# Attention scores as two products over all 128 rows, and the band mask in fp32r

## The chip, the cores and the metric

The kernel runs on one core of a Trainium2 chip. The metric is the device time of one execution in microseconds (us), the median of the runs shown; the kernel before takes 1642.43 us.

## The reference, cut to what matters

A two-layer backbone works on 256 context tokens followed by 256 latent tokens, 1024 channels each, all in float32. Each layer has three mixers side by side (differential attention, a gated recurrence, windowed attention), gates that merge them, an output projection and a squared-ReLU MLP. The change touches the scores of the two attentions:

```python
def diff_weights(q, k, lam):                 # differential attention, 4 heads x 2 parts of 64 channels
    s = jnp.einsum('bqhcd,bkhcd->bhcqk', q, k) * (DIFF_DIM ** -0.5)
    p = jax.nn.softmax(s, axis=-1)
    return p[:, :, 0] - lam * p[:, :, 1]
...
band = jnp.abs(kj - SWA_BLOCK - qi) <= WINDOW      # windowed attention, 8 query heads, 2 key heads of 64
s_win = jnp.einsum('bqhgd,bkhd->bhgqk', qn, kw) * scale
s_win = jnp.where(valid, s_win, MASK_VALUE)
s_ctx = jnp.einsum('bqhgd,bkhd->bhgqk', qn, k_c) * scale
```

Context queries see the 256 context keys; latent queries see all 512. The second layer needs latent queries alone.

## The kernel before, in words

**Products of split numbers.** A dense product is computed to nearly float32 precision from fp32r operands: each operand is stored as a high part (rounded to fp32r) and a low part (what rounding left). `mm_cm` (L240 to L251) and `mm_tm` (L253 to L263) issue three products per 128 rows: high x high, high x low, low x high. `weights` (L197) loads blocks of weights over SyncE's queue (SP) and splits them: ScalarE rounds (L227), VectorE subtracts (L228).

**The score operands.** A head has 64 channels, and two heads (or two parts of a head) share one 128-row tile. After the dense product, `rope` turns the latent columns on POOL (L907 to L909). `stack_q` (L911) builds for each half c a tile S: in the rows of that half the high part of the query (L917), in the other 64 rows its low part (L918). `stack_k` (L920) builds for each half a tile K1[c] that holds the high part of the key in both row halves (ScalarE, L928 and L929), and one tile KL for both halves, in which the rows of half c hold the low part of key c (VectorE, L930).

**The scores.** `scores` issues two products into one PSUM bank: S against K1[c] over all 128 rows (L937), which sums high x high and low x high, and then the rows of half c of S against the same 64 rows of KL (L938), high x low. The moving operand has 512 columns for a latent query tile and 256 for a context tile. In `swa_unit` a latent tile gets a third product (L1075): an identity against a 128x128 band of 0 and -1e30, both kept in bf16 in the tile `half`, added onto the 128 key columns that the window cuts.

**What follows.** In `diff_head` VectorE takes the row maximum (L977), ScalarE the exponential (L898), VectorE normalizes and subtracts the two parts (L980 to L983), TensorE transposes the weights (L989), ScalarE copies them (L991), TensorE multiplies with the values (L1002). In `swa_unit` the same is done with L1079 (maximum), L1090 (scaling), L1097 (transposes), L1100 and L1102 (copies) and L1110 (values, 64 columns of weights each); ScalarE and VectorE write the output split in two (L1116, L1117).

**What sets the order.** The code is traced in program order with generators run in turn: `run` steps two heads alternately, `pipeline` holds two window units in flight. A scheduler then puts the instructions of each engine in one fixed order, by priority and a model of times; blocks under `hp()` have a higher priority. So dense products of the next stage (blocks of w_in, gates, branch projections) stand between the score products on TensorE. Each engine works through its order strictly. Key stacks, splits of weights (L228) and maxima share VectorE's one queue.

**Buffers.** `R` is a pool of 22 units of 128x512 words. `get(k)` takes the k neighbouring units that were freed longest ago. `acts` (L892) takes the split outputs of a mixer, four pairs of units. Stacks take one unit per tile.

Of the kernel before, what the change touches and what calls it, by code (L numbers as in the profile page):

```python
# [13 lines left out]
BF16 = mybir.dt.bfloat16  # L14
AF = mybir.ActivationFunctionType
ALU = mybir.AluOpType
# [96 lines left out]
class Net:  # L113
    def __init__(self, ctx, tc, ins, out):
        self.tc, self.nc = tc, tc.nc
        self.I, self.out = ins, out
        nc = self.nc
        cp = ctx.enter_context(tc.tile_pool(name="cp", bufs=1))
        pp = ctx.enter_context(tc.tile_pool(name="pp", bufs=1, space=PSUM))

        def const(n, cols, dt=F32):
            return cp.tile([128, cols], dt, tag=n, name=n)

        self.cst = const("cst", C_END)
        self.msk = const("msk", SMALL * 32 + 128, I32)
        self.half = const("half", 3 * 128, BF16)
        self.prm = const("prm", 96)
        self.bT = const("bT", 96)
        self.M = [const(f"M{l}", 96) for l in range(DEPTH)]
        self.CA = const("CA", 256)  # L130
        self.sb = const("sb", 128)
        self.sl = const("sl", 256)
        self.hn = const("hn", 256)
        self.snk = const("snk", 32)
        self.lam = const("lam", 4)
        self.oml = const("oml", 8)
        self.nhalf = const("nhalf", 8)
        self.ones = const("ones", 32)
        self.yss = const("yss", 20)
        self.sm_t = const("sm", 512)  # L140
        self.sm_i = 0
        self.raw = const("raw", RAWS * 1024)
        self.whl = const("whl", 2 * 4096)
        self.h = const("h", 2 * 8 * T)
        nf, nr = 33, 22
        self.arf = const("arf", nf * UNIT)
        self.arr = const("arr", nr * UNIT)
        self.A = Arena(self.arf, 0, nf)
        self.R = Arena(self.arr, 0, nr)
        self.x = {}  # L150
        self.last_dma = None
        self.fence = [0, 0, []]
        self.exps = []
        self.pumps = []
        self.rate = 1
        self.ps = [pp.tile([128, 512], F32, tag=f"b{i}", name=f"b{i}") for i in range(8)]
        self.nd, self.np = 2, 7
        self.di = self.mi = self.wi = self.ri = 0
        self.ident = self.cst[:, C_ID:C_ID + 128]
        self.hact = [(r32(self.h[:, k * T:(k + 1) * T]), r32(self.h[:, (8 + k) * T:(9 + k) * T]))  # L160
                     for k in range(8)]
# [25 lines left out]
    def set_fence(self, ops, skip, count):  # L187
        """the splits of weight blocks skip .. skip + count - 1 from here on are traced behind ops"""
        self.fence = [skip, count, ops]
# [7 lines left out]
    def weights(self, pieces, rope=0, dst=None):  # L197
        """a block of 2048 columns, loaded in halves; pieces(half): (view fn of the half, source AP); the first `rope`
        columns, in groups of 64 (axis, half, 16), are taken as (half, axis, 16)"""
# [42 lines left out]
    def mm_cm(self, ps, w, nk, cc, act, t0, n, kt0=0, start=True, stop=True):  # L242
        """ps[128 channels, n tokens] = w[:, cc:cc+128]^T act"""
        nc = self.nc
        hi, lo = w
        for k in range(nk):
            xh, xl = act[kt0 + k]
            wh, wl = hi[:, k, cc:cc + 128], lo[:, k, cc:cc + 128]
            nc.tensor.matmul(ps, wh, xh[:, t0:t0 + n], start=start and k == 0, stop=False)  # L249
            nc.tensor.matmul(ps, wh, xl[:, t0:t0 + n], start=False, stop=False)  # L250
            nc.tensor.matmul(ps, wl, xh[:, t0:t0 + n], start=False, stop=stop and k == nk - 1)  # L251

    def mm_tm(self, ps, w, nk, c0, n, act, tt, kt0=0, start=True, stop=True):  # L253
        """ps[128 tokens, n] = act[:, tt]^T w[:, c0:c0+n]"""
        nc = self.nc
        hi, lo = w
        for k in range(nk):
            xh, xl = act[kt0 + k]
            xh, xl = xh[:, tt * 128:tt * 128 + 128], xl[:, tt * 128:tt * 128 + 128]
            wh, wl = hi[:, k, c0:c0 + n], lo[:, k, c0:c0 + n]  # L260
            nc.tensor.matmul(ps, xh, wh, start=start and k == 0, stop=False)  # L261
            nc.tensor.matmul(ps, xh, wl, start=False, stop=False)  # L262
            nc.tensor.matmul(ps, xl, wh, start=False, stop=stop and k == nk - 1)  # L263

# [34 lines left out]
    def setup_mixers(self):  # L299
# [10 lines left out]
        nc.vector.tensor_copy(self.half[:, 0:128], self.ident)  # L310
        nc.vector.tensor_copy(self.half[:, 128:384], self.cst[:, C_BAND:C_BAND + 256])
# [57 lines left out]
    def ada_late(self, l, groups, ahead=2):  # L369
        """the groups of layer l on the vector engine; each step loads for a later one"""  # L370
# [22 lines left out]
    def ada_acc(self, raw, k, acc):  # L393
        """sums over k of w * silu(c), by partition, one for each stream"""
# [50 lines left out]
    def mvec(self, l, s, i):  # L445
        """stream s: 0 latents, 1 context"""
        return self.M[l][:, s * 48 + i * 8:s * 48 + i * 8 + 8]

# [1 line left out]
    def rstd(self, ms, cols, add=True):  # L450
        """ms: mean squares, to which EPS is added unless it is in them"""
# [6 lines left out]
    def scale_vecs(self, l, sub, q=None):  # L458
        """of all channel tiles, or of q and 4 + q"""
# [11 lines left out]
    def first_norm(self):  # L471
        """normalized and transposed x, channel tile k -> [128, 512]"""
# [40 lines left out]
    def first_blocks(self, offs, evacs):  # L513
        """the first blocks of w_in[0]; channel tiles q and 4 + q are multiplied as soon as their modulation is known"""
# [45 lines left out]
    def prenorm(self, tt, yb):  # L560
        """x[tt] / rms, transposed: the PSUM tiles of channels 0..511 and 512..1023"""
# [24 lines left out]
    def modulate(self, tt, sv, tiles, yb, ops=(), quick=False):  # L586
        """the tiles of prenorm() to the activation of tokens tt; traced behind ops"""
# [36 lines left out]
    def post(self, tt, y, yss):  # L624
        """x += y / rms, where y already holds the gains; yss [128, 5]: the shares of y's quarters in the mean
        square, and EPS"""
# [10 lines left out]
    def tm_out(self, w, r0, act, y, yss, seqs, add, gains=None, after=None):  # L637
        """y[tt] (+)= act^T w[r0:r0 + 1024]; seqs: lists of (tokens, column blocks) worked through in turn; with gains,
        the mean squares of y are taken and y becomes y * gains(tt)"""
# [28 lines left out]
    def hgrn_dense(self, l, w, hp):  # L668
        """heads 2 hp and 2 hp + 1"""
# [59 lines left out]
    def tm_pair(self, w, off, dst=None):  # L729
        """buffers, token tiles [128, 256] in them, and the function that fills those of a range"""  # L730
# [14 lines left out]
    def hgrn_head(self, l, hd, s, v, gn, ys):  # L745
        """generator: one step of the chain at a time"""
# [116 lines left out]
    def readout(self, ps, tiles, gain, ys):  # L863
        """per-tile rms norm of ps[128 tokens, tile, 128], gain, transpose, split"""
# [27 lines left out]
    def acts(self, n):  # L892
        bufs = [self.R.get(2) for _ in range(n)]
        return bufs, [(r32(b[:, 0:T]), r32(b[:, T:2 * T])) for b in bufs]

# [4 lines left out]
    def rope(self, t):  # L900
        """in place on the latent half of t [128, 512]; 64-row heads hold (half, axis, 16)"""
# [10 lines left out]
    def stack_q(self, t, c, t0):  # L912
        """rows 64 c of t -> [128, tokens] with the high part there and the low part in the other rows"""
# [7 lines left out]
    def stack_k(self, t):  # L921
        """high parts of both row halves, each doubled; low parts"""
        nc = self.nc
        K1 = [self.R.get(1) for _ in range(2)]
        KL = self.R.get(1)
        for c in range(2):
# [3 lines left out]
            nc.vector.tensor_tensor(out=r32(KL[own, :]), in0=t[own, :], in1=K1[c][own, :], op=ALU.subtract)  # L930
        return K1, KL

    def scores(self, ps, S, c, tt, K1, KL, nk, stop=True):
        nc = self.nc
        own = slice(64 * c, 64 * c + 64)
        q = slice(tt * 128, tt * 128 + 128)
        nc.tensor.matmul(ps[:, 0:nk], r32(S[:, q]), r32(K1[c][:, 0:nk]), start=True, stop=False)  # L937
        nc.tensor.matmul(ps[:, 0:nk], r32(S[own, q]), r32(KL[own, 0:nk]), start=False, stop=stop)  # L938
# [19 lines left out]
    def diff_head(self, l, hd, q, k, v, ys):  # L958
# [37 lines left out]
        for b in S + K1 + [KL]:  # L996
            b.free()
# [61 lines left out]
    def swa_unit(self, l, tt, gp, S, K1, KL, v, ys):  # L1059
        """heads 2 gp, 2 gp + 1 of both groups for one token tile; column order (kv, g)"""  # L1060
# [8 lines left out]
        for i in range(4):  # L1069
# [3 lines left out]
            if tt >= 2:  # L1073
                k0 = 384 if tt == 2 else 256
                nc.tensor.matmul(ps[:, k0:k0 + 128], self.half[:, 0:128],  # L1075
                                 self.half[:, (tt - 1) * 128:tt * 128], start=False, stop=True)
# [46 lines left out]
    def gates(self, l, j, bufs=()):  # L1123
        """left as they are where the exponentials of a mixer run beside them; branch() takes the sigmoid then"""
# [18 lines left out]
    def branch(self, l, j, ys, gates, merged, last):  # L1143
        """merged += gates * (ys^T w_branch[j])"""
# [37 lines left out]
    def cm_blocks(self, loads, q0, skew, evac, done=lambda b: None, also=None):  # L1182
        """two channel tiles per block; skew: the first two blocks take the context half first, also()
        follows them in each half"""
# [32 lines left out]
    def pipeline(self, gens, depth):  # L1217
        """starts one generator per round, at most `depth` at a time"""
# [10 lines left out]
    def layer(self, l):  # L1229
# [5 lines left out]
        # token mixer  # L1235
# [29 lines left out]
        for b in list(S.values()) + K1 + [KL, sv]:  # L1265
            b.free()
# [39 lines left out]
        # channel mixer  # L1306
# [97 lines left out]
```

## Time and profile before

| | us |
|---|---|
| median of 3 runs | 1642.43 |
| lowest, highest run | 1640.19, 1645.79 |
| span of the profiled execution, first to last instruction | 1638.2 |
| TensorE matmuls busy in that span | 1596.6 (97%) |
| VectorE busy | 1082.4 (66%) |
| ScalarE busy | 784.5 (48%) |
| GpSimd (POOL) busy | 387.9 (24%) |

The profile holds one execution; the time around its span is known from the runs, which lie 2.0 to 7.6 us above it. PE is TensorE's matmuls, PEld its loads of weights (the stationary operand), which can run beside matmuls, DVE is VectorE, ACT is ScalarE. Matmuls are pipelined, so the durations of neighbours overlap; the distance from one start to the next tells what one occupies. Lines like L938 are lines of the kernel before.

### The profile page before, as it was taken

The page shows a single profiled execution, that of the slowest core. Times are in us where ns is not written, and L with a number is a line of the kernel's source. Part 1 is how long each engine was busy: PE and PEld are TensorE (multiplying, and loading weights), DVE is VectorE, ACT ScalarE, POOL GpSimd, SP SyncE. Part 2 cuts the span into 40 slices and gives each one's busy share as a digit, 9 for nine tenths or more (in the row PEclk, how much of TensorE's full clock was granted, in tenths as well). Part 3 has the DMA queues.
Part 4 walks back from the last instruction along what each step waited for, and adds up shares of the span by engine and source line. Part 5 has one row for each costly group of instructions (what it writes and reads, how often), then busy time and mean ns, then how long its engine had stood idle before and what let it go on. Part 6 is the DMA issues. An engine that isn't in the chain of part 4 may idle for free.

```text
span 1638.2 us, 30088 instructions
## 1 busy us (share of the span) xinstructions
PE 1596.6 (97%) x11806; PEld 1395.9 (85%) x11806; DVE 1082.4 (66%) x1974; ACT 784.5 (48%) x1648; POOL 387.9 (24%) x419
## 2 busy tenths in 40 slices
PE   6999999999999999999999999999999999989998
PEld 4788888787777679989898989999898888989998
DVE  4655534676466568777878756877768787765555
ACT  4443433455444457533324235754446655666554
POOL 1142415050410000310202011364455350121001
PEclk9999999999999999999999999999999999999999
DMA  9723243323432335465565524432434253436552
GB/s 279 227 79 116 79 142 103 93 63 116 132 97 55 106 113 184 149 208 174 174 187 186 177 82 143 141 104 78 130 104 104 76 157 104 155 121 188 182 181 91
DMA packets 234270, 220.26 MB, mean 134 GB/s; under 512 B 24400, under 2 KB 226320, under 8 KB 234128
## 3 DMA queue, kind: packets, MB, share of 16 engines
q1 hardware_dynamic: 234128, 218.34, 43.6%
q8 instruction: 92, 1.51, 0.4%
q14 instruction: 50, 0.41, 0.1%
HBM read 217.26 MB, written 1.05 MB: 133 GB/s over the span
## 4 chain that ended last, share of the span: by engine, by line
PE 85%; DVE 5%; POOL 4%; DMA 2%; issue 2%; ACT 2%; SPq 0%; DVEq 0%; POOLq 0%; ACTq 0%
PE b L249 15%; PE b L251 15%; PE b L250 15%; PE b L261 9%; PE b L263 8%; PE b L262 8%; PE b L938 2%; DMA arf<-in_w_ada_dram 1%; PE b L937 1%; POOL arf L907 1%; POOL arf L797 1%; PE b L1110 1%; PE b L365 1%; PE b L1097 1%; DVE whl L228 1%
## 5 line engine op out<-in xcount | busy, mean ns | idle before, releaser
L228 DVE TENSOR_TENSOR whl<-raw,whl 128x512 fp32r<-128x512 f32 x588 | 432.9, 757 | 217.3 <-ACT whl L227 205.1
L227 ACT CAST whl<-raw 128x512 fp32r<-128x512 f32 x588 | 356.3, 619 | 253.3 <-PE b L263 111.9
L249 PE MATMUL b<-h,whl 128*128 128x512 f32 (+1 forms) x1296 | 448.2, 347 | 0.4 <-ACT arf L741 0.2
L251 PE MATMUL b<-h,whl 128*128 128x512 f32 (+1 forms) x1296 | 446.1, 345 | 0.8 <-DVE whl L228 0.6
L250 PE MATMUL b<-h,whl 128*128 128x512 f32 (+1 forms) x1296 | 444.1, 343 | 0.0
L249 PEld LDWEIGHTS b<-h,whl 128*128 128x128 f32 x1296 | 247.0, 191 | 33.1 <-issue 2.7
L251 PEld LDWEIGHTS b<-h,whl 128*128 128x128 f32 x1296 | 246.3, 190 | 31.7 <-issue 3.4
L250 PEld LDWEIGHTS b<-h,whl 128*128 128x128 f32 x1296 | 246.4, 190 | 28.6 <-issue 3.3
L261 PE MATMUL b<-whl,arr 128*128 128x256 f32 x768 | 217.2, 284 | 0.0
L262 PE MATMUL b<-whl,arr 128*128 128x256 f32 x768 | 217.1, 283 | 0.0
L263 PE MATMUL b<-whl,arr 128*128 128x256 f32 x768 | 215.6, 283 | 1.0 <-DVE arr L1321 1.0
L1320 POOL TENSOR_TENSOR arf<-arf 128x256 f32<-128x256 f32 (+1 forms) x68 | 63.9, 939 | 425.1 <-ACT arr L1319 421.5
L261 PEld LDWEIGHTS b<-whl,arr 128*128 128x128 f32 x768 | 147.3, 192 | 1.3 <-DVE arf L653 0.8
L263 PEld LDWEIGHTS b<-whl,arr 128*128 128x128 f32 x768 | 146.6, 192 | 1.4 <-DVE arr L1321 1.4
L262 PEld LDWEIGHTS b<-whl,arr 128*128 128x128 f32 x768 | 147.4, 192 | 0.1
L261 PE MATMUL b<-whl,h 128*128 128x256 f32 x512 | 145.6, 286 | 0.0
L262 PE MATMUL b<-whl,h 128*128 128x256 f32 x512 | 145.4, 285 | 0.0
L263 PE MATMUL b<-whl,h 128*128 128x256 f32 x512 | 144.2, 285 | 0.0
L907 POOL TENSOR_TENSOR arf<-arf,cst 32x256 f32<-32x256 f32 x104 | 93.7, 901 | 204.9 <-DVE arf L983 80.9
L455 POOL TENSOR_TENSOR sm<-sm,nhalf 128x1 f32<-128x1 f32 (+2 forms) x42 | 32.3, 773 | 348.6 <-DVE sm L630 257.6
L404 DVE SCALAR_TENSOR_TENSOR arf<-arf,CA 128x1024 f32<-128x1024 f32 x84 | 110.0, 1355 | 5.3 <-DMA arf<-in_w_ada_dram 5.3
L261 PEld LDWEIGHTS b<-whl,h 128*128 128x128 f32 x512 | 97.8, 192 | 3.6 <-issue 1.2
(224 smaller groups left out, 2493.8 us busy)
## 6 DMA issues: line engine op xcount, KB each, us to landing
raw<-in_w_in_dram SPq DMA_DIRECT2D x110, 512.0 KB, 3.7
arf<-in_w_ada_dram SPq DMA_DIRECT2D x80, 512.0 KB, 4.7
raw<-in_w_mlp_down_dram SPq DMA_DIRECT2D x72, 512.0 KB, 3.9
raw<-in_w_mlp_up_dram SPq DMA_DIRECT2D x64, 512.0 KB, 3.8
raw<-in_w_out_dram SPq DMA_DIRECT2D x24, 512.0 KB, 3.4
arf<-in_w_ada_dram SPq DMA_DIRECT2D x32, 256.0 KB, 5.8
raw<-in_w_branch_dram SPq DMA_DIRECT2D x16, 512.0 KB, 3.7
raw<-in_w_in_dram SPq DMA_DIRECT2D x32, 128.0 KB, 2.9
```

What stands on the lines that cost most here:

```text
L227: self.behind(ops, lambda: nc.scalar.copy(r32(h), src))
L228: self.split_op = self.behind(ops, lambda: nc.vector.tensor_tensor(out=r32(l), in0=src, in1=h, op=ALU.subtract))
L249: nc.tensor.matmul(ps, wh, xh[:, t0:t0 + n], start=start and k == 0, stop=False)
L250: nc.tensor.matmul(ps, wh, xl[:, t0:t0 + n], start=False, stop=False)
L251: nc.tensor.matmul(ps, wl, xh[:, t0:t0 + n], start=False, stop=stop and k == nk - 1)
L261: nc.tensor.matmul(ps, xh, wh, start=start and k == 0, stop=False)
L262: nc.tensor.matmul(ps, xh, wl, start=False, stop=False)
L263: nc.tensor.matmul(ps, xl, wh, start=False, stop=stop and k == nk - 1)
L404: self.nc.vector.scalar_tensor_tensor(out=a[:, :], in0=raw[:, :], scalar=ca[:, k, s:s + 1], in1=a[:, :], op0=ALU.mult, op1=ALU.add)
L907: nc.gpsimd.tensor_tensor(out=b[o, 0:LAT], in0=x[i], in1=self.cst[i, C_RS:C_RS + LAT], op=ALU.mult)
L938: nc.tensor.matmul(ps[:, 0:nk], r32(S[own, q]), r32(KL[own, 0:nk]), start=False, stop=stop)
L1320: nc.gpsimd.tensor_tensor(out=r[:, c], in0=r[:, c], in1=r[:, c], op=ALU.mult)
```

## The change

`stack_k` makes two tiles KL[c] in place of one, each with the low part of key c in both row halves, which takes four subtractions per stack instead of two. The second score product then takes all 128 rows of S against all 128 rows of KL[c]; it adds low x low, which was left out before. The identity and the band are stored in fp32r in place of bf16. `acts` takes its four pairs as one block of eight units. Comments and docstrings are removed throughout; all lines move.

```diff
-        self.half = const("half", 3 * 128, BF16)
+        self.half = const("half", 3 * 128)
...
-        nc.vector.tensor_copy(self.half[:, 0:128], self.ident)
-        nc.vector.tensor_copy(self.half[:, 128:384], self.cst[:, C_BAND:C_BAND + 256])
+        nc.vector.tensor_copy(r32(self.half[:, 0:128]), self.ident)
+        nc.vector.tensor_copy(r32(self.half[:, 128:384]), self.cst[:, C_BAND:C_BAND + 256])
...
     def acts(self, n):
-        bufs = [self.R.get(2) for _ in range(n)]
-        return bufs, [(r32(b[:, 0:T]), r32(b[:, T:2 * T])) for b in bufs]
+        b = self.R.get(2 * n)
+        return [b], [(r32(b[:, 2 * i * T:(2 * i + 1) * T]), r32(b[:, (2 * i + 1) * T:(2 * i + 2) * T])) for i in range(n)]
...
     def stack_k(self, t):
         K1 = [self.R.get(1) for _ in range(2)]
-        KL = self.R.get(1)
+        KL = [self.R.get(1) for _ in range(2)]
         for c in range(2):
             own, oth = slice(64 * c, 64 * c + 64), slice(64 - 64 * c, 128 - 64 * c)
             nc.scalar.copy(r32(K1[c][own, :]), t[own, :])
             nc.scalar.copy(r32(K1[c][oth, :]), t[own, :])
-            nc.vector.tensor_tensor(out=r32(KL[own, :]), in0=t[own, :], in1=K1[c][own, :], op=ALU.subtract)
+            for o in (own, oth):
+                nc.vector.tensor_tensor(out=r32(KL[c][o, :]), in0=t[own, :], in1=K1[c][own, :], op=ALU.subtract)
         return K1, KL

     def scores(self, ps, S, c, tt, K1, KL, nk, stop=True):
         nc = self.nc
-        own = slice(64 * c, 64 * c + 64)
         q = slice(tt * 128, tt * 128 + 128)
         nc.tensor.matmul(ps[:, 0:nk], r32(S[:, q]), r32(K1[c][:, 0:nk]), start=True, stop=False)
-        nc.tensor.matmul(ps[:, 0:nk], r32(S[own, q]), r32(KL[own, 0:nk]), start=False, stop=stop)
+        nc.tensor.matmul(ps[:, 0:nk], r32(S[:, q]), r32(KL[c][:, 0:nk]), start=False, stop=stop)
...
-                nc.tensor.matmul(ps[:, k0:k0 + 128], self.half[:, 0:128],
-                                 self.half[:, (tt - 1) * 128:tt * 128], start=False, stop=True)
+                nc.tensor.matmul(ps[:, k0:k0 + 128], r32(self.half[:, 0:128]),
+                                 r32(self.half[:, (tt - 1) * 128:tt * 128]), start=False, stop=True)
```

Where the stacks are freed, `K1 + [KL]` becomes `K1 + KL`.

## Rows read from the trace of the kernel before

**Rows 1.** The page: busy time, share of the span and instructions of each engine.
```profile
PE 1596.6 (97%) x11806; PEld 1395.9 (85%) x11806; DVE 1082.4 (66%) x1974; ACT 784.5 (48%) x1648; POOL 387.9 (24%) x419
```

**Rows 2.** Windows: busy us of each engine per stretch, granted clock, DMA share, GB/s.
```profile
280.00:600.00 320.00, 319.73 (x1653) 236.75 (x1652) 189.57 (x402) 150.61 (x340) 51.84 (x62) 1.00 0.32 96
1225.00:1405.00 180.00, 177.55 (x1247) 152.50 (x1246) 136.53 (x259) 107.76 (x237) 58.43 (x67) 1.00 0.38 109
1230.00:1280.00 50.00, 48.84 (x310) 41.07 (x309) 42.68 (x72) 30.21 (x65) 23.93 (x26) 1.00 0.37 95
```

**Rows 3.** Matmul timeline: start, duration, line, out and in, shape; among ordinary products.
```profile
1240.25 0.40 PE L937 MATMUL b<-arr 128*128 128x512 f32 x1
1240.48 0.28 PE L251 MATMUL b<-h,whl 128*128 128x256 f32 x1
1240.60 0.28 PE L249 MATMUL b<-h,whl 128*128 128x256 f32 x1
```

**Rows 4.** Matmul timeline around two score groups of layer 0's windowed attention.
```profile
477.14 0.39 PE L251 MATMUL b<-arr,whl 128*128 128x512 f32 x1
477.46 0.50 PE L938 MATMUL b<-arr 64*128 64x512 f32 x1
477.89 0.23 PE L1075 MATMUL b<-half 128*128 128x128 bf16 x1
477.93 0.47 PE L937 MATMUL b<-arr 128*128 128x512 f32 x1
478.33 0.49 PE L938 MATMUL b<-arr 64*128 64x512 f32 x1
478.75 0.50 PE L249 MATMUL b<-arr,whl 128*128 128x512 f32 x1
479.09 0.39 PE L250 MATMUL b<-arr,whl 128*128 128x512 f32 x1
```

**Rows 5.** Timeline of weight loads (PEld) in the same stretch, with idle time before.
```profile
476.91 0.19 PEld L251 LDWEIGHTS b<-arr,whl 128*128 128x128 f32 x1
477.45 0.18 PEld L938 LDWEIGHTS b<-arr 64*128 64x128 f32 x1 [0.35 <-issue]
477.88 0.10 PEld L1075 LDWEIGHTS <-half 128*128 128x128 bf16 x1 [0.25 <-issue]
```

**Rows 6.** Instructions of line L938, and its engine's idle time ahead (us, times).
```profile
L938 PE MATMUL b<-arr x96: 277/492/502, 290.2 to 1383.0; 64*128 64x512 f32 x64, 64*128 64x256 f32 x32
...
  issue: 20.1, 71
```

**Rows 7.** Matmul timeline, a second score product of 256 columns in layer 0.
```profile
296.88 0.38 PE L938 MATMUL b<-arr 64*128 64x256 f32 x1
297.19 0.44 PE L989 MATMUL b<-cst,arf 128*128 128x128 f32 x2
297.38 0.48 PE L249 MATMUL b<-arr,whl 128*128 128x512 f32 x1
```

**Rows 8.** Matmul timeline, 128-column f32 products of layer 0.
```profile
341.45 0.61 PE L1002 MATMUL b<-arf 128*128 128x128 f32 x4
341.90 0.60 PE L989 MATMUL b<-cst,arf 128*128 128x128 f32 x4
```

**Rows 9.** Instructions of line L930: ns min/median/max.
```profile
L930 DVE TENSOR_TENSOR arr<-arf,arr x20: 672/689/1218, 276.3 to 1303.5; 64x512 fp32r<-64x512 f32 x20
```

**Rows 10.** VectorE and matmul timeline, where a stack ends close ahead of its scores.
```profile
313.16 0.69 DVE L930 TENSOR_TENSOR arr<-arf,arr 64x512 fp32r<-64x512 f32 x1
...
314.52 0.28 PE L937 MATMUL b<-arr 128*128 128x256 f32 x1
```

**Rows 11.** Matmul and ScalarE timeline: last read, first write of a mixer's outputs.
```profile
501.44 0.39 PE L251 MATMUL b<-arr,whl 128*128 128x512 f32 x1
...
510.61 0.27 ACT L1116 CAST arr<-b 128x128 fp32r<-128x128 f32 x1 [2.86 <-PE b L1110]
```

**Rows 12.** Windows, columns as in the second group: a stretch with stops.
```profile
1410.00:1450.00 40.00, 34.76 (x260) 33.37 (x259) 32.38 (x68) 25.46 (x62) 7.75 (x9) 0.92 0.48 152
```

More of the change, by code (lines that the diff above doesn't have):

```diff
@@ L13 @@
 I32 = mybir.dt.int32
-BF16 = mybir.dt.bfloat16
 AF = mybir.ActivationFunctionType
@@ L995, in diff_head @@
             yield
-        for b in S + K1 + [KL]:
+        for b in S + K1 + KL:
             b.free()
@@ L1264, in layer @@
         self.pipeline([self.swa_unit(l, tt, gp, S, K1, KL, sv, ys_c) for tt in reversed(tts) for gp in range(2)], 2)
-        for b in list(S.values()) + K1 + [KL, sv]:
+        for b in list(S.values()) + K1 + KL + [sv]:
             b.free()
```

## The prediction

> **What bounds the kernel now.** I read the busy shares first: TensorE's matmuls fill 97% of the span and VectorE 66% [rows 1]. As an average says little of a stage, the two attention stretches were cut out by windows: 280 to 600 us (layer 0) and 1225 to 1405 us (layer 1). TensorE is busy for 319.73 of 320 us and for 177.55 of 180 us, at a granted clock of 1.00, its upper level of 2.4 GHz [rows 2]. So there the matmul queue sets the pace: what a product occupies is paid, and what is taken from it comes back unless another engine is then late. VectorE is the next, and tightest in layer 1's differential attention, 42.68 of 50 us [rows 2].
>
> "Busy" hides how well the queue is filled, so the matmul timeline is read by the distance from one start to the next. A 512-column product on 128 rows costs 0.23 us among ordinary ones, a 256-column one 0.12 (1240.25 to 1240.48 to 1240.60, [rows 3]); that first product is L937 itself. Where L938 on 64 rows comes in, three distances grow [rows 4]: the one before it from 0.23 to 0.32 (477.14 to 477.46), its own to 0.43 (477.46 to 477.89), and that of the next full product to 0.34 (478.75 to 479.09). The weight loads say why: an ordinary load starts with the product before its own (the load at 476.91 serves the product of 477.14), while L938's starts at 477.45 with its product, after 0.35 us of idle [rows 4, 5]. The load queue was so held up ahead of 71 of the 96 L938, 20.1 us in all [rows 6].
>
> **The change part by part.**
> *Second score product on 128 rows (L938).* It keeps its 512 or 256 columns and its weights become the same 128x128 block that L937 loads. Its price becomes L937's among ordinary products, 0.23 or 0.12. Saved per product of 512 columns: 0.09 ahead + 0.20 of its own + 0.11 behind = 0.40. With 256 columns its own distance is 0.31 (296.88 to 297.19) instead of 0.12 [rows 7]; with 0.09 ahead and 0.10 behind, taken from the case of 512, that is 0.38. L938 is issued 96 times, 64 at 512 and 32 at 256 columns [rows 6]: 64 x 0.40 + 32 x 0.38 = 37.8. Where transposes follow instead of a product no delay is seen behind (297.19, two of them in 0.19 us, [rows 7]); I count 11 such places or ones followed by products of 32 or 64 columns, and take off 11 x 0.10 = 1.1. That leaves 36.7 us.
>
> *Band product in fp32r (L1075, 32 times: 2 token tiles x 2 x 4 heads x 2 layers).* It occupies 0.04 now (477.89 to 477.93) [rows 4]. No 128-column fp32r product is in the trace. Below, it stays at 0.04; above, it costs as much as a 512-column one, 0.23. I take the 128-column f32 products, four in 0.45 us, 0.11 each [rows 8]: they have its shape and an element as wide. So +0.07 x 32 = 2.2 us, between 0 and 6. Its weight load grows from 0.10 us towards the 0.19 of the load at 476.91 [rows 5]; I cost that at nothing, since an ordinary load lies beside the product before it. If that cover were gone it would cost 32 x 0.09 = 2.9 us. The Trainium skill (TensorE: Matmul & The Clock Gate, Weight-path perf modes) says that fast weight loading is for 128 weights of a type other than FP32; by it this part gives up a fast load. The two load lengths agree with that.
>
> Freed on the matmul queue: 36.7 - 2.2 = 34.5, say **34 us**.
>
> *Two more subtractions per key stack (L930).* Ten stacks get 20 more VectorE instructions of 64x512, median 0.69 and at most 1.22 us [rows 9] (the long ones fall where POOL runs rope): 14 to 24 us of VectorE time, for the most part beside other work. They also push back what is queued behind them, weight splits (L228) and the maxima (L977) for which exp waits. Mostly the stack ends well ahead of its scores. In some places it is close: the subtraction that starts at 313.16 ends at 313.85 and the first score of 256 columns follows at 314.52 [rows 10], 0.67 us, against 1.4 us added. Layer 1's differential stage, with 42.68 of 50 us, holds six of today's 20 and so gets six more, 4.1 to 7.3 us, while TensorE there gets faster; the work can slide into 1280 to 1300 us in part. I let 5 us come back as new waits there and in two or three close places; bounds none, and half of the 24.
>
> *Low parts in two buffers, outputs of a mixer in one block of eight units.* Going through the allocator's rule by hand, the pool of 22 units holds at most 20 at once in the attention stages. The outputs of the window attention now lie wholly on those of the differential attention; three of their four pairs did so before. The last product that reads these starts at 501.44 and the first write comes at 510.61 [rows 11], 9 us later. No cost. The setup's two casts and the removed comments: nothing.
>
> **Sum.** 34 - 5 = 29 us off the span of 1638.2, which gives 1609.2. The median shown lies 4.2 us above that span, so 1613.4: **1613 us**.
>
> **Rivals.**
> *Half goes into new waits.* TensorE, 7% faster in these stretches, meets the chain of maximum, exp and scaling that its own slowness covers now. For it: VectorE's share of 85% in one stage and the 0.67 us gap. Against it: today's idle time is 0.27 us in 320 and 2.45 in 180 [rows 2], so most results arrive well ahead. It gives back 17 us: 1625, between 1618 and 1635.
>
> *The full-height product is held up as well, so nothing is freed.* If a weight load could go ahead only beside a product on other rows, L938 would keep its 0.43 us; with the wider load and the band product 5 us would be added: 1647. Against it stand the ordinary products, all on 128 rows, whose loads do start one product ahead [rows 5]. The Trainium skill (TensorE: Matmul & The Clock Gate, The mechanism) has a rule of this kind, that loads overlap running matmuls only where the row group differs; the trace disagrees, with loads on the same 128 rows at a distance of 0.23 us.
>
> *Slower: the key stacks stop TensorE and its clock falls.* If at each of the ten stacks TensorE stood for both added subtractions at their longest, that is 10 x 2.44 = 24 us. Stops cost more than themselves: in 1410 to 1450 us TensorE idles 5.24 us and the mean granted clock is 0.92 [rows 12]; 16% of 40 us at 1.2 GHz instead of 2.4 would be 6.4 us, up to 3.2 of them lost, 0.6 per idle us. So 24 x 1.6 = 39 us against the 34: 1642.4 + 5 = 1647. It decides from 3.4 us per stack on, a stop of 2.1 us and its clock. Against it: all stacks but a few have other products queued between.
>
> **Chances.** Forecast 0.70, half given back 0.18, nothing freed 0.04, stops and clock 0.08; the last two shared out between no change (0.06) and slower (0.06). What can be told from no change here is 0.3%, 5 us. Faster 0.88. Range: below, 36.7 us with a band product at 0.04, no new wait and some us of scatter, 1601; above, half given back with a part of its spread, 1631.
>
> **What would show it.** L938's weight loads with no "issue" idle ahead of them; L938 at 0.23 to the next start, the product behind it too; L1075 at 0.11; L930 40 times; TensorE's idle time in the two stretches up by less than 5 us, at a clock of 1.00. The prediction is wrong if L938's loads still start with their products, or if the stretches, shorter in matmul time, are filled with waits for L930, L977 or L228.

## The result, and the profile after

The changed kernel takes **1622.66 us** (median of 4 runs, 1621.37 to 1623.33); the kernel before takes 1641.31 beside it (4 runs, 1639.38 to 1645.79). The ratio is 0.9884, with a 95% interval of 0.9868 to 0.9900: 18.7 us faster. Three executions of the runs below took 1932 us or more, in a slower state, and the medians leave them out. The forecast of 1613 was 9.7 us too low; the time lies inside the range and 2.3 us from the rival "half goes into new waits" (1625). Lines of the changed kernel carry the number of before minus one from L228 on (L936 and L937 are the two score products, L1074 the band), save for L930, the subtraction, which keeps its own.

First the page of the changed kernel, its busy times, which answer to [rows 1]:

```profile
PE 1569.2 (97%) x11806; PEld 1401.7 (86%) x11806; DVE 1091.5 (67%) x1994; ACT 782.5 (48%) x1648; POOL 387.8 (24%) x419
```

TensorE is busy 27.4 us less. The span, 1638.2 before and 1620.9 now, fell by only 17.3, so 10.1 us of the gain came back as idle time: span minus busy time was 41.6 and is 51.7.

**The score products did what was forecast.** The lines of L937 and L930 after (nanoseconds are minimum, median, maximum), which answer to [rows 6, 9]:

```profile
L937 PEld LDWEIGHTS b<-arr x96: 187/190/193, 289.8 to 1365.5; 128*128 128x128 f32 x96
L937 PE MATMUL b<-arr x96: 278/391/474, 289.9 to 1365.7; 128*128 128x512 f32 x64, 128*128 128x256 f32 x32
its engine sat idle before it (us, times) until:
...
L930 DVE TENSOR_TENSOR arr<-arf,arr x40: 674/687/1247, 275.6 to 1292.3; 64x512 fp32r<-64x512 f32 x40
```

Under "sat idle before it" nothing is left, where 20.1 us of "issue" in 71 places stood before. The matmul timeline after, around two score groups of layer 0's windowed attention, answers to [rows 4]:

```profile
470.99 0.39 PE L250 MATMUL b<-arr,whl 128*128 128x512 f32 x1
471.22 0.39 PE L937 MATMUL b<-arr 128*128 128x512 f32 x1
471.44 0.22 PE L1074 MATMUL b<-half 128*128 128x128 f32 x1
471.50 0.45 PE L936 MATMUL b<-arr 128*128 128x512 f32 x1
471.79 0.40 PE L937 MATMUL b<-arr 128*128 128x512 f32 x1
472.02 0.39 PE L248 MATMUL b<-arr,whl 128*128 128x512 f32 x1
472.25 0.39 PE L249 MATMUL b<-arr,whl 128*128 128x512 f32 x1
```

Read by starts, the product ahead of L937 takes 0.23 (470.99 to 471.22), L937 itself 0.22 and 0.23, the product behind it 0.23 (472.02 to 472.25). All three of the delays of before (0.32, 0.43, 0.34) are gone. The band product takes 0.06 and the product behind it 0.29, that is 0.06 over an ordinary one.

**Where the rest went** is read from the windows of the changed kernel. The columns are those of [rows 2]; the first two stretches are the two attention stretches at their new place, the next three lie inside them:

```profile
280.00:590.00 310.00, 305.76 (x1678) 242.21 (x1677) 200.04 (x422) 152.52 (x345) 52.93 (x62) 0.99 0.34 100
1209.00:1389.00 180.00, 171.37 (x1270) 159.15 (x1269) 141.15 (x271) 109.75 (x243) 60.37 (x69) 0.98 0.40 111
320.00:330.00 10.00, 7.68 (x35) 4.99 (x34) 9.89 (x24) 7.63 (x21) 0.72 (x1) 0.98 0.51 115
330.00:340.00 10.00, 10.00 (x43) 8.20 (x42) 4.50 (x7) 1.92 (x5) 8.67 (x12) 0.84 0.00 0
1250.00:1260.00 10.00, 5.62 (x33) 5.62 (x34) 9.71 (x17) 5.79 (x10) 4.16 (x5) 0.66 0.01 2
```

TensorE idles 4.24 us in the first stretch and 8.63 in the second, against 0.27 and 2.45 [rows 2]. In both bad places VectorE is full, 9.89 and 9.71 of 10 us, and the granted clock drops (0.84 behind the first, 0.66 in the second). In the first place TensorE's stops are short, 2.3 us in six; they end with exponentials (L897, four times), a scaling (L982) and an instruction of ScalarE (L951), and two of the exponentials had themselves waited for VectorE's maxima.

The largest stop stands in layer 1's differential attention. The matmul timeline after:

```profile
1247.81 0.28 PE L262 MATMUL b<-whl,h 128*128 128x256 f32 x1
1254.38 1.11 PE L988 MATMUL b<-cst,arf 128*128 128x128 f32 x4 [6.29 <-DVE arf L982]
...
1255.51 0.41 PE L261 MATMUL b<-whl,h 128*128 128x256 f32 x1
1255.72 0.42 PE L262 MATMUL b<-whl,h 128*128 128x256 f32 x1
...
1258.22 0.28 PE L262 MATMUL b<-whl,h 128*128 128x256 f32 x1
1258.34 0.28 PE L260 MATMUL b<-whl,h 128*128 128x256 f32 x1
```

In TensorE's order the transposes come next, and it waits 6.29 us for their input, the last scaling of the softmax (L982). After the stop a 256-column product takes 0.21 (1255.51 to 1255.72) instead of 0.12: the granted clock is at its lower level, 1.2 GHz, until 1258.1. That is twelve distances, 12 x 0.09 = 1.1 us. The four transposes and the product behind them take 1.13 (1254.38 to 1255.51) where 0.45 [rows 8] and 0.12 would do, another 0.5 or so. The stop and its clock cost 7.9 us in all.

Why L982 is so late stands on VectorE's timeline of the same stretch:

```profile
1242.15 0.68 DVE L976 TENSOR_REDUCE sm<-b 128x1 f32<-128x512 f32 x1
1246.02 1.56 DVE L916 CAST arr<-arf 64x256 fp32r<-64x256 f32 x2 [3.19 <-POOL arf L908]
1247.61 0.90 DVE L917 TENSOR_TENSOR arr<-arf,arr 64x256 fp32r<-64x256 f32 x1
1248.54 0.17 DVE L979 RECIPROCAL sm<-sm 128x2 f32<-128x2 f32 x1
...
1249.40 1.48 DVE L916 CAST arr<-arf 64x256 fp32r<-64x256 f32 x2
1250.92 0.90 DVE L980 TENSOR_SCALAR arf<-arf,sm,lam 128x512 f32<-128x512 f32 x1
1251.85 1.69 DVE L917 TENSOR_TENSOR arr<-arf,arr 64x256 fp32r<-64x256 f32 x2
1253.58 0.75 DVE L982 SCALAR_TENSOR_TENSOR arf<-arf,sm 128x512 f32<-128x512 f32 x1
```

and on ScalarE's, where the sum of the exponentials, the reciprocal's input, is read out:

```profile
1242.87 0.69 ACT L897 ACTIVATE arf<-b,sm 128x512 f32<-128x512 f32 x1 [2.42 <-DVE sm L976]
1243.45 0.19 ACT L897 ACTIVATION_READ_ACCUMULATOR arf<-b,sm 128x1 f32 x1
```

The reciprocal could have run at 1243.6. In VectorE's fixed order it stands behind two casts and a subtraction of the next heads' query stack, the first of which (L916) waits 3.19 us for POOL's rope (L908). Five more instructions of that stack stand ahead of the two scalings (L980, L982). None of L930 is in this chain.

**By stage.** The first product of each score pair (L937 before, L936 after) cuts the timeline into stages, from the start of the first such product to that of the last. They repeat to about 0.1 us from run to run where nothing was changed (once to 0.4); the setup (289 to 294 us to the first score) and the stretch between the layers (642 to 646) scatter by more than that. "Freed" is counted from distances of starts, the medians of before minus those of after: 0.40 for a 512-column product; 0.38 with 256 columns in the differential attention (0.09 ahead, 0.19 own, 0.10 behind) and 0.29 on average in the windowed one; 0.31 where a band product follows (0.09 ahead, 0.20 own, 0.02 for the band and what is behind it).

```
us, first to last score pair        before   after   change   freed by distances       given back
layer 0 differential                111.09  105.62    -5.5    16x0.40 + 16x0.38 = 12.5       7.0
layer 0 windowed                    108.45   99.11    -9.3    16x0.31 + 16x0.29 =  9.6       0.3
layer 1 differential                 67.39   68.88    +1.5    16x0.40           =  6.4       7.9
layer 1 windowed                     44.21   39.78    -4.4    16x0.31           =  5.0       0.6
all the rest                        1307.1  1307.5    +0.4                                   0.4
```

Less 1.1 for the places where transposes follow, 32 us were freed, and about half of it came back: the windowed attention kept its gain, the differential attention lost most of it.

### The profile page after: what moved, and what is told of

The parts are those of the page before. It is cut to its first block, busy times and chain, and to the rows that moved or that the text cites. A ratio compares the mean times of both kernels' runs of the same rounds, so it can differ in the third digit from the quotient of the medians.

```text
span 1620.9 us, 30093 instructions
## 1 busy us (share of the span) xinstructions
PE 1569.2 (97%) x11806; PEld 1401.7 (86%) x11806; DVE 1091.5 (67%) x1994; ACT 782.5 (48%) x1648; POOL 387.8 (24%) x419
## 4 chain that ended last, share of the span: by engine, by line
PE 84%; DVE 4%; POOL 4%; DMA 2%; ACT 2%; issue 2%; SPq 1%; DVEq 0%; POOLq 0%; ACTq 0%
PE b L248 15%; PE b L249 15%; PE b L250 15%; PE b L260 9%; PE b L261 9%; PE b L262 9%; DMA arf<-in_w_ada_dram 1%; POOL arf L906 1%; PE b L364 1%; POOL arf L796 1%; PE b L1109 1%; PE b L936 1%; PE b L1096 1%; DVE whl L227 1%; PE b L937 1%
```

## The experiments

Two accounts of the loss stood against each other. One: the added subtractions cost it, as work or through the order that they bring about. The other: a faster TensorE runs into VectorE's chain whether or not subtractions are added. Each run below changes what its title says (with two low tiles the block of eight goes along, as the pool then needs it); times are medians, ratios are to the kernel before on the same chip.

**The block of eight units alone.**

```diff
     def acts(self, n):
-        bufs = [self.R.get(2) for _ in range(n)]
+        b = self.R.get(2 * n)
...
```

> Kernel before, with the outputs of a mixer in one block of eight units and nothing else. All theories: the placement is free, 1641 us, within 5 us, with TensorE's starts as before (L938 at 0.43 us). If placement or the new order that the scheduler makes of it counts, it moves by more than 5 us either way.

1640.59, ratio 0.9997 [0.9988, 1.0006]. It costs nothing, as forecast; the windowed stage of layer 0 stays at 108.45 us.

**The band in fp32r alone**, beside second score products on 64 rows as before.

```diff
-        self.half = const("half", 3 * 128, BF16)
+        self.half = const("half", 3 * 128)
```

> Kernel before, with identity and band in fp32r and nothing else. By the prediction's term the band product goes from 0.04 to 0.11 us: 32 x 0.07 = 2.2 us slower, 1643.5. By the trace of after the product takes 0.06 and 0.05 more behind it, 0.11 to 0.12 together, where before it took 0.04 and 0.09 behind it: no change, 1641. If its wider weight load were exposed, up to 1646.

1644.51, ratio 1.0016 [1.0006, 1.0026], 2.6 us slower by the ratio; the two windowed stages grow by 1.34 and 1.40 (109.79, 45.60), 2.7 us together. The matmul timeline of this run:

```profile
478.00 0.50 PE L938 MATMUL b<-arr 64*128 64x512 f32 x1
478.43 0.33 PE L1075 MATMUL b<-half 128*128 128x128 f32 x1
478.59 0.45 PE L937 MATMUL b<-arr 128*128 128x512 f32 x1
478.87 0.39 PE L249 MATMUL b<-arr,whl 128*128 128x512 f32 x1
```

Behind a 64-row product the fp32r band takes 0.16 and the product behind it 0.28. Behind a full-height one it took 0.06. So the step was right in size (2.2) for the old neighbours, but not for the new ones.

**The score products alone**: the change with the band left in bf16.

> Kernel before, with the full-height score product (low parts in two tiles, four subtractions per stack) and the block of eight, which the pool needs then; band in bf16 as before. Theory A (full-height products free some 30 us, a stop of TensorE in layer 1 takes 8 back): all of the gain is here, 1620 to 1625, with a stop of some 6 us in layer 1's differential stage if the order there is the same. Theory B (each product frees less than priced): the same time with no such stop. Rival (the band carries a good part of the gain): 1630 or more.

1624.82, ratio 0.9898 [0.9880, 0.9917]. The windowed stages (99.45 and 40.03) are only 0.34 and 0.25 us longer than with the fp32r band: beside full-height products fp32r is not the dearer one. The weight loads of the band in this run say why:

```profile
L1075 PEld LDWEIGHTS <-half x32: 95/96/99, 467.8 to 1367.7; 128*128 128x128 bf16 x32
...
  issue: 8.2, 31
```

A load half as long (0.096 against 0.19 us) is still held up ahead of 31 of the 32, although all products around it now have 128 rows. The stop of 6.3 us for L983 is here too: the band has no part in it.

**No added subtractions**: full height against the one tile KL as before, band in fp32r. The product then adds a term that the scores do not have, the query's low part times the low part of the other half's key.

```diff
-        nc.tensor.matmul(ps[:, 0:nk], r32(S[own, q]), r32(KL[own, 0:nk]), start=False, stop=stop)
+        nc.tensor.matmul(ps[:, 0:nk], r32(S[:, q]), r32(KL[:, 0:nk]), start=False, stop=stop)
```

> Kernel before, with fp32r band and the score product over all 128 rows of S against all 128 rows of the ONE tile KL, so that the low part of the query meets the low part of the other half's key; no added subtraction, no second tile, no block of eight. If the added subtractions are what takes the missing 10 us (VectorE too full), the time is 1611 to 1614. If the stop comes of the order on VectorE alone (casts of the next heads ahead of the last scaling), it stays: 1619 to 1623. If each product frees less than priced, 1621 to 1623 without a stop.

1619.28, ratio 0.9865 [0.9842, 0.9889]. Layer 1's differential stage takes 64.98 us, 3.9 less than in the changed kernel, and its wait for L982 there is 1.9 us instead of 6.3. Layer 0's takes 107.50, 1.9 more, but it holds eight 128-column products more than there, and the stretch behind it is shorter: counted on to the first windowed score it is 178.12 us, against 177.86 in the changed kernel and 183.57 before. So layer 0 loses as much as in the changed kernel although no subtraction was added, while layer 1 loses less: both accounts hold a part. In its window of 320 to 330 us VectorE is as full as after the change (9.75 of 10; 8.27 before).

**The changed kernel with another order in layer 1**: the stacks of the second pair of heads are placed behind the last scalings of the first pair, which `self.scaled` holds.

```diff
-        S = [self.stack_q(q, c, q0) for c in range(2)]
-        K1, KL = self.stack_k(k)
+        ops = self.scaled if l and hd > 1 else []
+        S = [self.behind(ops, lambda: self.stack_q(q, c, q0)) for c in range(2)]
+        K1, KL = self.behind(ops, lambda: self.stack_k(k))
...
```

> Kernel after, with one order added: in layer 1, VectorE's work on the query and key stacks of the second pair of heads is queued behind the last scalings of the first pair. Theory A (TensorE's 6.3 us stop comes of VectorE standing at a cast that waits for POOL's rope, with the last reciprocal and scalings queued behind it): the stop falls under 2 us, the half clock behind it goes too, 6 to 8 us are gained, 1614 to 1617. Theory B (VectorE has too much work there): the stop moves to the scores of the second pair, 1620 to 1624.

1622.96 (three executions), ratio 0.9881 [0.9864, 0.9897]. The stage got 3.8 us shorter (68.88 to 65.05), but the median shows no gain; in the profiled run the setup and the stretch between the layers are each 1.7 us longer, which lies within the scatter given above. The stop did not vanish, it halved and moved. The matmul timeline, then ScalarE's:

```profile
1258.12 1.76 PE L1004 MATMUL b<-arf 128*128 128x128 f32 x8 [2.75 <-ACT arf L993]
```

```profile
1255.48 0.62 ACT L929 CAST arr<-arf 64x512 fp32r<-64x512 f32 x1 [4.80 <-POOL arf L910]
...
1257.39 0.59 ACT L993 COPY arf<-b 128x512 f32<-128x512 f32 x1
```

Now the copy of the transposed weights (L993) stands in ScalarE's order behind the key casts (L929, L930), and the first of these waits 4.80 us for the same rope on POOL. The cure for one queue showed the same fault in the next.

**The same order without added subtractions.**

> The kernel with one shared tile KL, full-height products and fp32r band (no added subtraction), with the same order added in layer 1. It had 5.1 us of idle time of TensorE for the last scalings in three places, 2.4 the longest. Theory A: the places in layer 1 go, 1.5 to 3 us gained, 1616 to 1618. If the order was of no account there: 1619.

1614.25, ratio 0.9833 [0.9819, 0.9848]. Layer 1's differential stage is 61.61, 5.8 below before: of the 6.4 us freed there nearly all is kept.

**The added subtractions alone**: two tiles and four subtractions per stack, but the product still on 64 rows.

```diff
+            for o in (own, oth):
+                nc.vector.tensor_tensor(out=r32(KL[c][o, :]), in0=t[own, :], in1=K1[c][own, :], op=ALU.subtract)
...
-        nc.tensor.matmul(ps[:, 0:nk], r32(S[own, q]), r32(KL[own, 0:nk]), start=False, stop=stop)
+        nc.tensor.matmul(ps[:, 0:nk], r32(S[own, q]), r32(KL[c][own, 0:nk]), start=False, stop=stop)
```

> Kernel before with the 20 added subtractions and the second tile alone (and the block of eight, which the pool needs then): the second product still takes 64 rows of it. Theory A (the subtractions cost nothing of themselves; the freed TensorE time uncovers waits): 1641 to 1643, idle time up by less than 2 us. Theory B (they cost some 10 us through VectorE's queue): 1646 to 1651.

1647.88, ratio 1.0044 [1.0027, 1.0060]: 6.2 us over the 1641.65 of the kernel before beside it, 7.2 by the ratio. I had held that they cost next to nothing where TensorE is slow; that fell. By stage: layer 0 differential +1.6, layer 1 differential +3.0, from there to the windowed scores +2.1, middle +1.3 (the last within that stretch's scatter). TensorE's waits in this run:

```profile
PE b L990 <- DVE arf L984: 2.1, 2, 1.5
```

So the longest wait for the last scaling (L984 in this kernel), the one in layer 1, is at 1.5 us, up from 1.2 before, with TensorE as slow as ever; new in that stage is a wait of 1.7 us for the copy of the transposed weights (L992, ScalarE).

**The order alone, in the kernel before.**

> Kernel before with the order added in layer 1 and nothing else. TensorE waits there 1.16 us for the last scaling in the kernel before. Theory A (the same order stood in before and was covered by the slower products): 1 us gained at most, 1640 to 1641. If the order by itself is worth 6 us or more, 1635 or less.

1638.95, ratio 0.9984 [0.9972, 0.9996]. The stage gains 0.75 us (67.39 to 66.64). While TensorE was slow, the order that this one replaces cost under 1 us; with the faster one it cost 3 to 4. The scheduler's own order is not the same in the three kernels, though. VectorE's timeline before, then in the run without added subtractions, at the first casts of the next heads' query stack:

```profile
1255.08 1.04 DVE L917 CAST arr<-arf 64x256 fp32r<-64x256 f32 x2 [0.82 <-POOL arf L909]
```

```profile
1240.70 1.03 DVE L917 CAST arr<-arf 64x256 fp32r<-64x256 f32 x2 [1.46 <-POOL arf L909]
```

Before, two casts, two subtractions and a weight split stand ahead of the last scaling; without added subtractions, two casts and a split; in the changed kernel all eight instructions of the query stack, with 3.19 us of waiting. So the price of a like order with a faster TensorE is shown by the run without added subtractions; in the changed kernel the order itself is a worse one as well.

**The order in both layers**, first without added subtractions, then in the changed kernel.

```diff
-        ops = self.scaled if l and hd > 1 else []
+        ops = self.scaled if hd > 1 else []
```

> As the run with one shared tile KL, fp32r band and the order added in layer 1, but with the order in both layers. Without it layer 0's differential attention, 107.9 us from first to last score, has a stop of 2.4 us for a last scaling (half clock behind it) that stands on VectorE behind query casts and subtractions of the second pair. Theory A (that order is the cause there too): the stop goes, the stretch takes 104 to 106 us, 1611 to 1613 in all. Theory B (VectorE has too much work there whatever the order): the wait moves to the second pair's scores or to the values, 107 to 108 us, 1614.

1613.67 (1610.58 to 1614.81), ratio 0.9835 [0.9820, 0.9849]; not told apart from the same with layer 1 alone.

> Kernel after with the order in both layers. In layer 0 the kernel after has its waits in 320 to 330 us, where VectorE is busy for 9.89 of 10 us, with work of the first pair itself, and not behind the second pair's casts. So both theories expect no gain in layer 0: 105 to 106 us from first to last score of its differential attention; layer 1 as with the order there alone, 65 us. 1618 to 1623 in all.

1618.19, ratio 0.9864 [0.9848, 0.9881]. These two were timed side by side, and what differs is the second low tile (its twenty subtractions, and the block of eight): 4.5 us. In layer 0's differential stage they take 106.18 and 105.78, no less than the changed kernel's 105.62. The order by which layer 1 gains does next to nothing for layer 0: counted on to the first windowed score it moves that stretch by 0.8 us down and 0.5 up. The second run (layer 1's stage at 65.15) shows in the whole what the order in layer 1 alone did not: by the ratios it is 3.3 us below the changed kernel. One of the waits that remain in layer 0, in the run without added subtractions:

```profile
357.53 0.33 PE L882 MATMUL b<-cst,arf 128*128 128x128 f32 x1 [1.56 <-DVE arf L876]
```

It is for the norm behind the attention, again on VectorE.

## Why the prediction was right in sign and too large in size

- **The second score product** (34.5 us freed by forecast with the band, 32.4 by the distances). Right at 512 columns, to 0.01 us in each of the three distances, and right with 256 columns in layer 0's differential attention, the 0.09 "ahead" included, which was taken from the case of 512. The matmul timeline before, ahead of the L938 of [rows 7], then the same place after:

```profile
296.67 0.28 PE L937 MATMUL b<-arr 128*128 128x256 f32 x1
```

```profile
295.75 0.28 PE L936 MATMUL b<-arr 128*128 128x256 f32 x1
295.87 0.28 PE L937 MATMUL b<-arr 128*128 128x256 f32 x1
295.98 0.38 PE L988 MATMUL b<-cst,arf 128*128 128x128 f32 x2
```

  Before, L937 takes 0.21 (296.67 to 296.88) and L938 0.31; after, the two take 0.12 and 0.11. In layer 0's windowed attention most of the 256-column pairs stand beside products of f32 operands (L364, L1096, L1109), a case that the forecast did not look at: 0.29 came free there, 16 x 0.09 = 1.4 us less.
- **The band** (+2.2 forecast). +2.6 alone, with 64-row neighbours; beside full-height products its own distance and the delay behind it make 0.11 to 0.12 (0.06 + 0.06 in the timeline after), and 0.13 before (0.04 own, 0.09 behind). The 0.11 behind the 64-row product, which I took off also where the band follows it, was the band's delay and mostly stays. The two errors nearly cancel: 0.40 - 0.07 = 0.33 by forecast at such a place and 0.31 measured, 0.6 us over 32 places.
- **The rival "nothing freed"** fell. Weight loads on the same 128 rows do start one product ahead, and L937's are now among them. The Trainium skill (TensorE: Matmul & The Clock Gate, The mechanism) says in one sentence that loads overlap running matmuls only where the row group differs; the trace disagrees, with 96 loads of L937 and no idle time ahead of them. What was held up in the kernel before were loads next to a change of rows. The Trainium skill (TensorEngine Tiling (Array Packing), Key Properties) says that a change of the tiling mode drains TensorE; the 0.40 us per product that went away agree with a cost of that kind, and no run here shows the drain itself.
- **The block of eight, the setup's casts**: nothing, as forecast.
- **The step that failed: "I let 5 us come back".** The forecast priced the give-back by the added subtractions only, and by places where they come close to their scores. Measured: those subtractions cost 6 to 7 us by themselves, with nothing else changed. Beside full-height products, the pairs of runs with and without them differ by 3 us (0.9884 against 0.9865), 8 (0.9881 against 0.9833) and 4.5 (timed side by side). By stretch this is clearer. In layer 1, from the first differential to the first windowed score (112.50 us before, 114.35 after), they cost 4.6 to 5.1 in each of these four comparisons; in layer 0, counted likewise, 1.7 by themselves and between -0.5 and 0.9 beside full-height products. On top of that a faster TensorE spends its cover sooner. In layer 1 the scheduler's order costs 3.1 to 3.4 with the faster TensorE, counted likewise, and 0.8 with the slow one; without that order and without added subtractions the stretch is 106.33, and nearly all of the 6.4 us freed is kept. In the changed kernel the two together went with a stop of 6.29 us and 1.6 of clock. In layer 0 some 11.4 us were freed (12.5 less the 1.1), and every kernel with full-height products keeps only 5.1 to 5.9 of them, with added subtractions or without. In the changed kernel that is 3.5 us more idle time and, at a mean clock of 0.84 over 10 us (3.2 us of it at half speed), up to 1.6 of clock. The loss of cover, the rival's mechanism, had a chance of 0.18 on the ground that idle time was 0.27 and 2.45 us [rows 2]. Idle time says that the chain was covered, but not by how much.
- **The rival "slower: stops and clock"** has its mechanism in the trace at two places, not ten, so its price was far off.
- **The signs to look for**: no "issue" idle, 0.23 and L930 40 times came true. L1074 at 0.11 did only together with the delay behind it. Idle time in the two stretches went up by 10.2 us, not under 5. The wait named for a failure (L930, L977, L228) was the wrong one: the long wait was for L982 (L983 before), which is held behind the stack's other instructions, L916 and L917.

What stays open: why the whole run with the order in layer 1 alone shows nothing of its stage's 3.8 us (scatter of its three executions is the likely reason, not a shown one), and what would have to go first in layer 0's differential stage: no run takes its loss away, so that VectorE is the cause there is argued and not shown. One of TensorE's waits there, 1.5 us at 387 us in the changed kernel, is for a load of modulation weights from memory.

## What to carry to other kernels

A lone product with half the rows among full-height ones cost 0.20 us more of its own here and as much again in delays ahead and behind; fill its rows up, but from data that are there, since VectorE instructions added beside the bottleneck can cost part of what is won (about 5 us in layer 1, little in layer 0). Here filling from the shared tile, with the next heads' stacks ordered behind the running softmax, gives 1613.7 to 1614.3 against 1622.7, at the price of one more term of the size of low x low. Before forecasting a gain on the busiest engine, follow the in-order queue of each partner at the places where it is nearly full and look for an instruction that waits for a third engine ahead of one that the busiest engine needs: in layer 1 the time freed did not come back at such a place.

## What the runs showed of the hardware that was not expected

- The cost of a small product hangs on its neighbour's height: the fp32r band took 0.16 behind a 64-row product and 0.06 behind a 128-row one.
- A bf16 weight load of 0.096 us between fp32r products of the same height was held up nonetheless, 8.2 us over 31 of 32 places, where the fp32r load of 0.19 us goes ahead as others do. The changed kernel's timeline of weight loads shows the latter: the band's load (L1074) starts at 467.91, one product ahead, while the band product itself starts at 468.14:

```profile
467.68 0.19 PEld L937 LDWEIGHTS b<-arr 128*128 128x128 f32 x1
467.91 0.19 PEld L1074 LDWEIGHTS b<-half 128*128 128x128 f32 x1
```
